# Merged last output parts, a power for the reciprocal root, weight remainders on VectorE, head chains first, buffers moved

## The chip, the cores and the metric

One core of a Trainium2 chip runs the whole program in one launch. The metric is the device time of an execution in microseconds (us). The engines are TensorE (PE, with its weight loads PEld), VectorE (DVE), ScalarE (ACT), GpSimd (POOL) and SyncE (SP, which issues most DMAs). Tiles lie in SBUF; matmuls write PSUM banks of 512 float32 a partition.

## The reference, cut to what matters

Two transformer blocks on one sequence of 512 tokens, width 1024, in float32.

```python
# first block
xn = rmsnorm(h, norm_mix_g)
proj = xn @ w_in                      # q, k, v (512 each), u, gate (512 each), 8 forget logits
log_f = log_sigmoid(proj[..., -8:] + b_forget)
c = cumsum(log_f, axis=1)             # logits = q k / 8 + c_i - c_k, causal; softmax; times v: 8 heads
u, vg = gelu(uv)                      # vg: rmsnorm in groups of 64, mixed in chunks of 128 tokens
h = h + concat(att, u * mixed) @ w_out
h = h + conv_ffn(rmsnorm(h, norm_ffn_g))      # up to 2 x 2816, causal conv of 3, silu(g) * a, down
x = rmsnorm(h, norm_final_g)
# second block
h = modulate(rmsnorm(x), shift, scale)        # shift, scale, gates = silu(c) @ w_ada + b_ada
# latent attention (8 heads of 96) and banded attention with relative bias (8 heads of 64)
x = x + g_a * (concat(o_mla, o_ca) @ w_out)
x = x + g_m * conv_ffn(modulate(rmsnorm(x)))
```

## The kernel before, in words

Activations are kept feature-major as 8 tiles of 128 features x 512 tokens. Every product is computed in three matmuls: each operand is split into a rounded part (`hi`, or `h`) and a remainder (`lo`, or `l`), and hi·hi, hi·lo and lo·hi are added up in PSUM. A triple of matmuls 512 wide stands for one 128 x 128 block of weights.

**Weights.** `make_plan` (L270) lists all pieces of weights in the order in which they are used, each up to 128 x 1024. `load_split` (L327) loads one (SP's queue), casts it to `whi` on ACT (L340) and subtracts to get `wlo` (L341), on POOL where the plan says `pool=True`, else on DVE. There are 3 buffers for the raw pieces, 4 for `whi`, 4 for `wlo`; `prefetch` asks for a piece two pieces ahead of its use. In the first block `w_v` is on DVE; `w_g1` (3 pieces), `w_qk` tiles 0, 4, 1, 5 (one piece each), `w_g0` (2), `w_u` (4) and the other four of `w_qk` are on POOL. `gemm_fm` uses the weights as the stationary operand, `gemm_tm` uses the activations as the stationary one and the weights as the moving one.

**Order.** TensorE's order is written by the program: it runs in the order in which the code emits matmuls. On the other engines a scheduler orders what is ready, by the order of emission unless a priority is given. Work is emitted by generators that yield an estimate of their TensorE time; a `Fill` runs generators until a given estimate is used up. `attention` (L609) emits per step: the scores of one strip of 128 queries, half of the filler, the transposes of the strip before, the other half, the values of the strip before that. Filler is the projections still to do, the spatial gating and the output product; a second `Fill`, `bg`, emits gating work for DVE, POOL and ACT.

**First block, start.** `v`, then `g1` (gate columns and the forget logits), then `qk0`. From the logits ACT and DVE make log f (L1183 to L1194). `cumulate` (L1196) sums it over tokens in 8 matmuls and writes `cum` on ACT and DVE (L1202, L1203). `head(h)` (L1224) splits q and k of one head (`stack`, L650: `qs`, `kh`, `kl`), and picks the head's row out of `cum` with one matmul, whose copy `ch` and masked sum `cm` are the bias of the strips.

**Output product.** `gemm_part` (L393) multiplies two of the eight feature tiles at a time, so x is added to in four parts. `out_tail` (L416) does parts 2 and 3 for the first 256 tokens, then, woven with the norm of those tokens, part 2 and part 3 for the last 256: for each of 8 output tiles 6 matmuls of part 2 and a DVE addition to x (L837, second block L914), later 6 of part 3 and another. Part 3 needs the last pair of heads, which is marked ready in halves as `mix[3, 0]` and `mix[3, 1]`.

**Norms.** `norm_steps` sums squares with 8 small matmuls, calls `rstd` (L501), spreads the result over partitions with `to_rows` (4 matmul records), then `norm_apply` scales. `rstd` is called six times: for each half of the two feed-forward norms and twice in `stats` (L864) between the blocks. It does two DVE operations (L506, L507) and on POOL one (L510) and three Newton rounds of four (L515, L517 twice, L519).

**Memory.** In SBUF, from low to high: descriptor scratch of 16384 bytes a partition, constants, `wraw`, `whi`, `wlo` (4096 bytes a buffer), the activations `act` (8 x 4096), x (8 x 2048), small tiles `sm` (4928 in all, of which 16 of 32 bytes for `rstd`), `acc` (4 x 1024), and above them the pools of a stage: in the feed-forward stages `gh` and `gl`, the 44 operands of the down product, 2048 bytes each.

Of the kernel before, what the change touches and what calls it, by code (L numbers as in the profile page):

```python
# [10 lines left out]
F32 = mybir.dt.float32  # L11
# [8 lines left out]
P = 128  # L20
# [203 lines left out]
LOOK = 2  # L224
HALVES = (slice(0, 256), slice(256, 512))


class Kernel:
# [41 lines left out]
    def make_plan(self):  # L270
        i, plan = self.i, []

        def fm(name, tiles, kt0=0, nk=KT, pool=False, last=None):
            for n in tiles:
                for p in self.fm_pieces(i[name], n, kt0, nk):
                    plan.append((p, pool, None))
            if last:
                plan[-1] = plan[-1][:2] + (last,)

        def tm(name, n, nk=KT, pool=True, last=None, per=None):  # L280
            for p in self.tm_pieces(i[name], n, nk, per):
                plan.append((p, pool, None))
            if last:
                plan[-1] = plan[-1][:2] + (last,)

        def parts(name, dest):
            for p in range(4):
                for g in range(2):
                    plan.append((i[name][p, g], False, dest.get((p, g))))
# [37 lines left out]
    def load_split(self, src, pool, dest):  # L327
# [87 lines left out]

    def out_tail(self, w, mix, evac, evac_last, norm_a):  # L416
# [6 lines left out]
        yield from weave(norm_a, chain(self.gemm_part(w, 2, mix, evac, b, hl2),  # L423
                                       self.gemm_part(w, 3, mix, evac_last, b, hl3, lambda: (3, 1) in mix)))
# [76 lines left out]
    def rstd(self, ms, scale, bias, pool=True):  # L501


        nc = self.nc
        x, y, a, r = (self.sm.tile([P, 2], F32, tag="rstd" + nm, name="rstd", bufs=4) for nm in "xyar")
        nc.vector.tensor_scalar(out=x, in0=ms, scalar1=scale, scalar2=bias, op0=ALU.mult, op1=ALU.add)  # L506
        nc.vector.tensor_scalar(out=y.bitcast(I32), in0=x.bitcast(I32), scalar1=-0.5,  # L507
                                scalar2=float(0x5F3759DF), op0=ALU.mult, op1=ALU.add)
        g = nc.gpsimd if pool else nc.vector
        g.tensor_scalar(out=x, in0=x, scalar1=-0.5, scalar2=None, op0=ALU.mult)  # L510
        cols = (slice(0, 1), slice(1, 2))
        for j in range(3):
            out = r if j == 2 else y
            if pool:
                g.tensor_tensor(out=a, in0=y, in1=y, op=ALU.mult)  # L515
                for c in cols:
                    g.tensor_scalar(out=a[:, c], in0=a[:, c], scalar1=x[:, c], scalar2=1.5, op0=ALU.mult,  # L517
                                    op1=ALU.add)
                g.tensor_tensor(out=out, in0=a, in1=y, op=ALU.mult)  # L519
            else:  # L520
                for c in cols:
                    g.scalar_tensor_tensor(out=a[:, c], in0=y[:, c], scalar=x[:, c], in1=y[:, c],
                                           op0=ALU.mult, op1=ALU.mult)
                g.scalar_tensor_tensor(out=out, in0=a, scalar=1.5, in1=y, op0=ALU.add, op1=ALU.mult)
        return r
# [248 lines left out]
    def run(self):  # L774
# [9 lines left out]
        self.accp = self.pool("acc", 4)  # L784
        self.psn = 0
# [38 lines left out]
        nc.gpsimd.dma_start(out=self.pos, in_=i["pos"])  # L824

# [167 lines left out]
    def block1_mix(self, xn, x, evac, evac_last, norm_a):  # L993
# [143 lines left out]
        def qk(pr):  # L1137
            def ev(n, ps, cs):
                if n < 4:
                    qf[pr] = two.tile([P, 512], F32, tag="qf", name="qf")  # L1140
                    nc.vector.scalar_tensor_tensor(out=qf[pr], in0=ps, scalar=-0.125, in1=rrow,
                                                   op0=ALU.mult, op1=ALU.mult)
                else:
                    kf[pr] = two.tile([P, 512], F32, tag="kf", name="kf")
                    nc.vector.tensor_tensor(out=kf[pr], in0=ps, in1=rrow, op=ALU.mult)
# [37 lines left out]
        nc.scalar.activation(out=la, in_=lf, func=AF.Abs)  # L1183
        nc.scalar.activation(out=la, in_=la, func=AF.Exp, scale=-1.0)
        nc.scalar.activation(out=la, in_=la, func=AF.Ln, bias=1.0)

        lf2 = self.pp.tile([P, 4, 64], F32, tag="p", name="lf2")
        nc.gpsimd.memset(lf2, 0.0)
        lfh, lfl = (stk.tile([P, 4, 64], F32R, tag="st", name="lf" + z) for z in "hl")
        for o in (0, 32):  # L1190
            nc.vector.scalar_tensor_tensor(out=lf2[:, :, o:o + 8], in0=lf, scalar=0.0, in1=la, op0=ALU.min,
                                           op1=ALU.subtract)
        nc.vector.tensor_copy(lfh, lf2)
        nc.vector.tensor_tensor(out=lfl, in0=lf2, in1=lfh.bitcast(F32), op=ALU.subtract)  # L1194
# [488 lines left out]
```

## Time and profile before

| | |
|---|---|
| median of 3 runs | 1263.24 us (1260.85, 1263.3, 1263.24) |
| the profiled execution | 1260.37 us, its span 1258.7 us |
| TensorE busy | 1210.9 us, 96% of the span, 6730 matmul records |
| VectorE, ScalarE, GpSimd busy | 810.2, 537.5, 207.2 us |
| mean granted TensorE clock | 0.986 |
| first block up to its feed-forward stage | about 0 to 243 us |
| feed-forward stage of the first block | about 243 to 613 us |
| second block up to its feed-forward stage | about 613 to 890 us |
| feed-forward stage of the second block | about 890 to 1258 us |

A row of the timeline gives the start, the length, the engine, the line, what is written from what, and in brackets the idle time of the engine before it with what ended it. Lengths of matmuls overlap, as they are pipelined; the distance of their starts is their rate. PEclk is the granted clock: 1.00 is 2.4 GHz, 0.50 is 1.2 GHz.

### The profile page before, as it was taken

The numbers are of one execution on the slowest core, as the hardware profiler recorded it, in microseconds if no ns is written. First come the engines' busy times: TensorE is split into PE (matmuls) and PEld (weight loads), VectorE is DVE, ScalarE is ACT, GpSimd is POOL, SyncE is SP. The second block draws the span as 40 slices with busy tenths as digits, with TensorE's granted clock in tenths as the row PEclk, the third lists the DMA queues.
The fourth block names the chain that finished last, engine by engine and source line by source line (L and its number), as shares of the span: only waits on it lengthen the run. The fifth ranks groups of instructions, "written<-read, shape, count | busy, mean of one in ns | idle before, by whom it ended". The sixth has DMA issues, their size and how long they took to land.

```text
span 1258.7 us, 17548 instructions
## 1 busy us (share of the span) xinstructions
PE 1210.9 (96%) x6730; PEld 1050.3 (83%) x6730; DVE 810.2 (64%) x1550; ACT 537.5 (43%) x964; POOL 207.2 (16%) x281
## 2 busy tenths in 40 slices
PE   9969999999999999999898999899999999999998
PEld 6868878898888888888898987789888888888887
DVE  6456877788778887533566889766676665563321
ACT  5435544454434443223344556664554444442110
POOL 2655700410000000000354342300400000000000
PEclk9979999999999999999999999999999999999999
DMA  7211221236565656533121221100142222233330
GB/s 236 86 65 51 85 84 43 76 118 191 182 196 200 201 196 189 168 104 113 56 68 55 69 96 59 52 23 29 34 134 101 99 87 99 101 92 101 115 111 17
DMA packets 40035, 131.59 MB, mean 105 GB/s; under 512 B 4608, under 2 KB 5504, under 8 KB 39952
## 3 DMA queue, kind: packets, MB, share of 16 engines
q1 hardware_dynamic: 31536, 102.64, 25.0%
q10 hardware_dynamic: 8208, 27.27, 6.7%
q8 instruction: 52, 0.85, 0.3%
q0 software_dynamic: 208, 0.57, 0.2%
q14 instruction: 31, 0.25, 0.1%
HBM read 128.37 MB, written 2.10 MB: 104 GB/s over the span
## 4 chain that ended last, share of the span: by engine, by line
PE 81%; DVE 8%; POOL 6%; ACT 3%; issue 2%; DMA 1%; SPq 0%; POOLq 0%; ACTq 0%; DVEq 0%
PE mm L362 72%; PE s L362 4%; PE o L362 3%; PE s L598 2%; POOL wlo L341 2%; DVE wlo L341 1%; DVE kl L663 1%; POOL gelu L1072 1%; DMA x<-in_xT_dram 1%; ACT p L589 1%; POOL gelu L1073 0%; DVE s L585 0%; DVE uv L1077 0%; PE s L689 0%; POOL sqg L1085 0%
## 5 line engine op out<-in xcount | busy, mean ns | idle before, releaser
L362 PE MATMUL mm<-xnh,whi 128*128 128x512 f32 (+1 forms) x832 | 313.0, 376 | 0.1
L362 PE MATMUL mm<-xnl,whi 128*128 128x512 f32 (+1 forms) x832 | 311.7, 375 | 0.4 <-POOL xnl L554 0.4
L362 PE MATMUL mm<-xnh,wlo 128*128 128x512 f32 (+1 forms) x832 | 311.4, 374 | 0.0
L340 ACT CAST whi<-wraw 128x1024 fp32r<-128x1024 f32 (+4 forms) x194 | 191.9, 991 | 270.3 <-PE mm L362 242.8
L341 DVE TENSOR_TENSOR wlo<-wraw,whi 128x1024 fp32r<-128x1024 f32 (+3 forms) x166 | 190.6, 1157 | 168.9 <-ACT whi L340 168.3
L362 PEld LDWEIGHTS mm<-xnh,wlo 128*128 128x128 f32 x832 | 157.4, 189 | 28.0
L362 PEld LDWEIGHTS mm<-xnh,whi 128*128 128x128 f32 x832 | 157.4, 189 | 27.8 <-issue 0.4
L362 PEld LDWEIGHTS mm<-xnl,whi 128*128 128x128 f32 x832 | 157.5, 189 | 27.6 <-POOL xnl L554 0.6
L362 PE MATMUL mm<-gh,whi 128*128 128x512 f32 (+1 forms) x384 | 143.0, 372 | 1.1 <-DVE x L927 0.6
L362 PE MATMUL mm<-gh,wlo 128*128 128x512 f32 (+1 forms) x384 | 142.0, 370 | 0.0
L362 PE MATMUL mm<-gl,whi 128*128 128x512 f32 (+1 forms) x384 | 140.9, 367 | 0.0
L723 DVE SCALAR_TENSOR_TENSOR cv<-mm,cols,cv 128x510 f32<-128x510 f32 (+1 forms) x176 | 130.4, 745 | 2.6 <-ACT cv L721 1.2
L362 PE MATMUL mm<-whi,xnh 128*128 128x256 f32 (+3 forms) x304 | 96.6, 318 | 2.4 <-ACT vv L1036 1.6
L362 PE MATMUL mm<-whi,xnl 128*128 128x256 f32 (+3 forms) x304 | 94.0, 309 | 0.1
L362 PE MATMUL mm<-wlo,xnh 128*128 128x256 f32 (+3 forms) x304 | 93.8, 309 | 0.2 <-DVE wlo L341 0.2
L988 DVE CUSTOM_DVE_ANT_0 wada<-wada,cs,cols 128x1024 f32<-128x1024 f32 x48 | 61.5, 1280 | 34.9 <-DMA wada<-in_w_ada_dram 34.9
L362 PEld LDWEIGHTS mm<-gh,wlo 128*128 128x128 f32 x384 | 72.1, 188 | 13.5
L362 PEld LDWEIGHTS mm<-gh,whi 128*128 128x128 f32 x384 | 72.3, 188 | 13.1 <-DVE x L927 0.8
L362 PEld LDWEIGHTS mm<-gl,whi 128*128 128x128 f32 x384 | 72.1, 188 | 12.9
L362 PE MATMUL mm<-mix,whi 128*128 128x256 f32 (+1 forms) x288 | 75.9, 352 | 4.3 <-ACT vm L1551 2.6
L589 ACT ACTIVATE p<-s,st 128x128 f32<-128x128 f32 (+1 forms) x96 | 50.7, 528 | 64.6 <-DVE st L585 49.3
L738 ACT ACTIVATE cv<-cv 128x512 f32<-128x512 f32 x44 | 27.8, 632 | 116.4 <-DVE cv L723 116.3
(313 smaller groups left out, 1930.8 us busy)
## 6 DMA issues: line engine op xcount, KB each, us to landing
wraw<-in_w_up_dram SPq DMA_DIRECT2D x88, 512.0 KB, 3.5
wada<-in_w_ada_dram ACTq DMA_DIRECT2D x48, 512.0 KB, 3.7
wraw<-in_w_down_dram SPq DMA_DIRECT2D x32, 512.0 KB, 3.5
wraw<-in_w_out_dram SPq DMA_DIRECT2D x16, 512.0 KB, 3.3
wraw<-in_w_down_dram SPq DMA_DIRECT2D x16, 384.0 KB, 3.2
wraw<-in_w_qk_dram SPq DMA_DIRECT2D x8, 512.0 KB, 3.5
wraw<-in_w_v_dram SPq DMA_DIRECT2D x8, 256.0 KB, 4.9
x<-in_xT_dram SPq DMA_DIRECT2D x8, 256.0 KB, 6.6
```

The source lines that it names most:

```text
L340: nc.scalar.copy(hi[:, :n], raw[:, :n])
L341: (nc.gpsimd if pool else nc.vector).tensor_tensor(out=lo[:, :n], in0=raw[:, :n], in1=hi[:, :n].bitcast(F32), op=ALU.subtract)
L362: self.nc.tensor.matmul(out, lhsT, rhs, start=start, stop=stop, **kw)
L589: nc.scalar.activation(out=p[:, :nk], in_=s[:, :nk], func=AF.Exp, bias=st[:, len(parts) - 1:len(parts)], scale=-1.0, accum_out=hd["sums"](qi))
L598: self.nc.tensor.transpose(s[:, c], p[:, c], self.ident)
L663: nc.vector.tensor_tensor(out=kl[o], in0=k[a], in1=kh[a].bitcast(F32), op=ALU.subtract)
L723: nc.vector.scalar_tensor_tensor(out=t[:, d:], in0=ps[:, :512 - d], scalar=w[2 - d], in1=t[:, d:], op0=ALU.mult, op1=ALU.add)
L738: nc.scalar.activation(out=gate, in_=gate, func=AF.Silu)
L988: nc.vector.tensor_tensor_reduce(out=w, in0=w, in1=self.cs, scale=1.0, scalar=self.col("b_ada_2", n), op0=ALU.mult, op1=ALU.add, accum_out ...
L1072: nc.gpsimd.tensor_tensor(out=t, in0=v, in1=v, op=ALU.mult)
```

## The change

1. **Merged parts.** In `out_tail` parts 2 and 3 of the last 256 tokens become one product: 12 matmuls for each output tile, then one addition to x. It starts when `mix[3, 1]` is marked.
2. **Power for rstd.** `rstd` becomes one DVE operation and one POOL operation, a power with exponent -0.5.
3. **VectorE remainders.** `wlo` of `w_g1`, `w_g0` and `w_qk` tiles 0, 4, 1, 5 is computed on DVE: 9 pieces.
4. **Priority.** The evacuations of q and k, log f (L1183 to L1194), the two writes of `cum` and the preparation of each head of the first block are emitted with a priority 40 places ahead of their own.
5. **Moved buffers.** Each buffer of `whi` and `wlo` is 1088 elements instead of 1024, pieces of token-major weights narrower than 384 columns start 48 elements (192 bytes) into it, a pad of 16 elements lies at the start of `acc`, and the descriptor scratch is 8192 bytes.

```diff
+SKEW, GPAD = 192, 16
+AHEAD = 40
...
         def tm(name, n, nk=KT, pool=True, last=None, per=None):
+            skew = SKEW // 4 if n < 384 else 0
             for p in self.tm_pieces(i[name], n, nk, per):
-                plan.append((p, pool, None))
+                plan.append((p, pool, None, skew))
...
         tm("w_v", 512, pool=False, per=1)
-        tm("w_g1", 264)
-        fm("w_qk", [0, 4], pool=True)
-        fm("w_qk", [1, 5], pool=True)
-        tm("w_g0", 256)
+        tm("w_g1", 264, pool=False)
+        fm("w_qk", [0, 4])
+        fm("w_qk", [1, 5])
+        tm("w_g0", 256, pool=False)
...
-            hi = self.whi.tile([P, 1024], F32R, tag="whi", name="whi")
-            lo = self.wlo.tile([P, 1024], F32R, tag="wlo", name="wlo")
+            hi = self.whi.tile([P, 1088], F32R, tag="whi", name="whi")[:, skew:]
+            lo = self.wlo.tile([P, 1088], F32R, tag="wlo", name="wlo")[:, skew:]
...
+    def gemm_parts(self, parts, x, evac, cs, hls, ready):
+        while not ready():
+            yield 0
+        todo = [(hl, q, k) for p, hl in zip(parts, hls) for q, k in enumerate(PARTS[p])]
+        for n in range(KT):
+            g, j = divmod(n, 4)
+            ps = self.bank()
+            o = ps[:, cs]
+            for m, (hl, q, k) in enumerate(todo):
+                hi, lo = hl[g]
+                ws = slice((2 * j + q) * P, (2 * j + q + 1) * P)
+                xh, xl = (t[:, cs] for t in x[k])
+                self.mm(o, hi[:, ws], xh, m == 0, False)
+                self.mm(o, hi[:, ws], xl, False, False)
+                self.mm(o, lo[:, ws], xh, False, m == len(todo) - 1)
+                yield 650 * (cs.stop - cs.start) // 512
+            evac(n, ps, cs)
...
-        yield from weave(norm_a, chain(self.gemm_part(w, 2, mix, evac, b, hl2),
-                                       self.gemm_part(w, 3, mix, evac_last, b, hl3, lambda: (3, 1) in mix)))
+        yield from weave(norm_a, self.gemm_parts((2, 3), mix, evac_last, b, (hl2, hl3), lambda: (3, 1) in mix))
...
     def rstd(self, ms, scale, bias, pool=True):
-        nc = self.nc
-        x, y, a, r = (self.sm.tile([P, 2], F32, tag="rstd" + nm, name="rstd", bufs=4) for nm in "xyar")
...
+        r = self.sm.tile([P, 2], F32, tag="rstd", name="rstd", bufs=4)
+        self.nc.vector.tensor_scalar(out=r, in0=ms, scalar1=scale, scalar2=bias, op0=ALU.mult, op1=ALU.add)
+        self.nc.gpsimd.tensor_tensor(out=r, in0=r, in1=self.nhalf, op=ALU.pow)
         return r
...
         self.accp = self.pool("acc", 4)
+        nc.gpsimd.memset(self.accp.tile([P, GPAD], F32, tag="pad", name="pad", bufs=1), 0.0)
...
+        self.nhalf = c.tile([P, 2], F32, name="nhalf")
+        nc.gpsimd.memset(self.nhalf, -0.5)
...
             def ev(n, ps, cs):
-                if n < 4:
...
+                with self.tc.high_priority(offset=AHEAD):
+                    if n < 4:
...
-        nc.scalar.activation(out=la, in_=lf, func=AF.Abs)
...
+        with self.tc.high_priority(offset=AHEAD):
+            nc.scalar.activation(out=la, in_=lf, func=AF.Abs)
...
-            nc.scalar.copy(cum, cp)
-            nc.vector.tensor_tensor(out=cum[32:64], in0=cp[32:64], in1=cum[32:64].bitcast(F32),
-                                    op=ALU.subtract)
+            with self.tc.high_priority(offset=AHEAD):
+                nc.scalar.copy(cum, cp)
+                nc.vector.tensor_tensor(out=cum[32:64], in0=cp[32:64], in1=cum[32:64].bitcast(F32),
+                                        op=ALU.subtract)
...
             def f(_):
+                fill.upto(f"qk{h // 2}") if h > 1 else None
+                with self.tc.high_priority(offset=AHEAD):
+                    return prepare(h)
+
+            def prepare(h):
                 pr, odd = divmod(h, 2)
-                fill.upto(f"qk{pr}") if pr else None
...
-    nc = _bacc.Bacc("TRN2", target_bir_lowering=False, num_devices=1)
+    nc = _bacc.Bacc("TRN2", target_bir_lowering=False, num_devices=1, dynamic_dma_scratch_size=8192)
```

## Rows read from the trace of the kernel before

**Rows 1.** The page: engines' busy time, and the granted clock in 40 slices.
```profile
PE 1210.9 (96%) x6730; PEld 1050.3 (83%) x6730; DVE 810.2 (64%) x1550; ACT 537.5 (43%) x964; POOL 207.2 (16%) x281
...
PEclk9979999999999999999999999999999999999999
```

**Rows 2.** Waits of PE, whole span: who waited for whom, us, times, longest.
```profile
PE s L598 <- ACT p L589: 10.1, 9, 2.4
PE mm L362 <- DVE cum L1203: 9.7, 1, 9.7
...
PE r L362 <- POOL rstd L519: 2.5, 1, 2.5
...
PE mm L362 <- POOL rstd L519: 1.3, 1, 1.3
PE mm L362 <- DVE x L914: 1.3, 1, 1.3
```

**Rows 3.** Timeline of PE around the wait for `cum`.
```profile
60.33 0.22 PE L362 MATMUL mm<-tri,lfl 128*64 128x128 f32 x1
...
73.75 0.79 PE L362 MATMUL mm<-cum,pick 64*128 64x512 f32 x1 [9.72 <-DVE cum L1203]
```

**Rows 4.** Stretches: length, busy time of each engine, PEclk, DMA share, GB/s.
```profile
64.00:73.70 9.70, 0.03 (x1) 0.00 (x0) 9.02 (x16) 4.71 (x7) 7.62 (x6) 0.63 0.18 57
73.70:80.20 6.50, 6.45 (x15) 4.76 (x16) 3.66 (x3) 0.59 (x1) 3.15 (x2) 0.50 0.30 102
...
609.30:612.70 3.40, 3.40 (x18) 3.40 (x17) 2.45 (x6) 2.38 (x5) 0.65 (x1) 0.50 0.02 5
```

**Rows 5.** Timeline of DVE from the first gate to `cum`.
```profile
41.85 0.43 DVE L1077 SCALAR_TENSOR_TENSOR uv<-gelu,uv 128x256 f32<-128x256 f32 x1 [0.49 <-ACT gelu L1076]
...
45.05 2.01 DVE L1077 SCALAR_TENSOR_TENSOR uv<-gelu,uv 128x256 f32<-128x256 f32 x1 [0.54 <-ACT gelu L1076]
...
59.66 2.48 DVE L660 TENSOR_TENSOR qs<-qf,qs 64x512 fp32r<-64x512 f32 x1 [1.03 <-ACT qs L659]
...
68.32 3.53 DVE L663 TENSOR_TENSOR kl<-kf,kh 64x512 fp32r<-64x512 f32 x2 [0.35 <-ACT kh L662]
71.87 1.10 DVE L660 TENSOR_TENSOR qs<-qf,qs 64x512 fp32r<-64x512 f32 x1
73.01 0.68 DVE L1203 TENSOR_TENSOR cum<-mm,cum 32x512 fp32r<-32x512 f32 x1
```

**Rows 6.** The same stretch: two remainders on POOL, and all of them.
```profile
44.12 2.65 POOL L341 TENSOR_TENSOR wlo<-wraw,whi 128x1024 fp32r<-128x1024 f32 x1
...
59.20 2.40 POOL L341 TENSOR_TENSOR wlo<-wraw,whi 128x1024 fp32r<-128x1024 f32 x1 [3.27 <-ACT whi L340]
...
L341 POOL TENSOR_TENSOR wlo<-wraw,whi 128x1024 fp32r<-128x1024 f32 (+2 forms) x8 | 18.5, 2308 | 7.6 <-ACT whi L340 7.5
```

**Rows 7.** Lines of DVE, whole span: remainders of 1024 columns.
```profile
L341 DVE TENSOR_TENSOR wlo<-wraw,whi 128x1024 fp32r<-128x1024 f32 x137 | 166.8, 1228 | 118.8 <-ACT whi L340 118.2
```

**Rows 8.** Timelines of PE and DVE at the end of the first output product.
```profile
231.49 1.00 PE L362 MATMUL o<-vv,pt 128*128 128x64 f32 x8
...
232.53 0.42 DVE L681 TENSOR_TENSOR att<-o,sums 128x256 f32<-128x256 f32 x1 [0.69 <-PE o L362]
...
242.06 0.98 PE L362 MATMUL mm<-mix,wsplit 128*128 128x256 f32 x6 [2.09 <-DVE x L837]
```

**Rows 9.** Timelines of DVE and POOL in `rstd` between the blocks.
```profile
604.20 1.23 DVE L341 TENSOR_TENSOR wlo<-wraw,whi 128x1024 fp32r<-128x1024 f32 x1
...
604.38 1.12 POOL L510 TENSOR_SCALAR rstd<-rstd 128x2 f32<-128x2 f32 x1 [343.18 <-DVE rstd L507]
...
608.63 0.19 POOL L519 TENSOR_TENSOR rstd<-rstd 128x2 f32<-128x2 f32 x1
```

**Rows 10.** Stretches of 512-wide matmuls: up product, then down product (columns as Rows 4).
```profile
300.00:400.00 100.00, 100.00 (x443) 82.84 (x442) 80.64 (x112) 41.95 (x56) 0.00 (x0) 1.00 0.59 191
500.00:590.00 90.00, 90.00 (x395) 73.89 (x394) 39.58 (x57) 27.45 (x43) 0.00 (x0) 1.00 0.43 131
```

More of the change, by code (lines that the diff above doesn't have):

```diff
@@ L275, in fm @@
                 for p in self.fm_pieces(i[name], n, kt0, nk):
-                    plan.append((p, pool, None))
+                    plan.append((p, pool, None, 0))
             if last:
-                plan[-1] = plan[-1][:2] + (last,)
+                plan[-1] = plan[-1][:2] + (last, 0)
         def tm(name, n, nk=KT, pool=True, last=None, per=None):
+            skew = SKEW // 4 if n < 384 else 0
             for p in self.tm_pieces(i[name], n, nk, per):
-                plan.append((p, pool, None))
+                plan.append((p, pool, None, skew))
             if last:
-                plan[-1] = plan[-1][:2] + (last,)
+                plan[-1] = plan[-1][:2] + (last, 0)
         def parts(name, dest):
@@ L288, in parts @@
                 for g in range(2):
-                    plan.append((i[name][p, g], False, dest.get((p, g))))
+                    plan.append((i[name][p, g], False, dest.get((p, g)), 0))
         def ffn(up, down, last=None):
@@ L325, in make_plan, with load_split @@
         self.ada_left, self.pools, self.before = [], {}, []
-    def load_split(self, src, pool, dest):
+    def load_split(self, src, pool, dest, skew):
         nc, n = self.nc, src.shape[-1]
@@ L1138, in ev @@
             def ev(n, ps, cs):
-                if n < 4:
[L1140 to L1145, printed above, removed]
+                with self.tc.high_priority(offset=AHEAD):
+                    if n < 4:
+                        qf[pr] = two.tile([P, 512], F32, tag="qf", name="qf")
+                        nc.vector.scalar_tensor_tensor(out=qf[pr], in0=ps, scalar=-0.125, in1=rrow,
+                                                       op0=ALU.mult, op1=ALU.mult)
+                    else:
+                        kf[pr] = two.tile([P, 512], F32, tag="kf", name="kf")
+                        nc.vector.tensor_tensor(out=kf[pr], in0=ps, in1=rrow, op=ALU.mult)
             return self.gemm_fm(i["w_qk"], [pr, 4 + pr], xn, ev)
@@ L1181, in block1_mix @@
         both(pre)
-        nc.scalar.activation(out=la, in_=lf, func=AF.Abs)
[L1184 to L1194, printed above, removed]
+        with self.tc.high_priority(offset=AHEAD):
+            nc.scalar.activation(out=la, in_=lf, func=AF.Abs)
+            nc.scalar.activation(out=la, in_=la, func=AF.Exp, scale=-1.0)
+            nc.scalar.activation(out=la, in_=la, func=AF.Ln, bias=1.0)
+            lf2 = self.pp.tile([P, 4, 64], F32, tag="p", name="lf2")
+            nc.gpsimd.memset(lf2, 0.0)
+            lfh, lfl = (stk.tile([P, 4, 64], F32R, tag="st", name="lf" + z) for z in "hl")
+            for o in (0, 32):
+                nc.vector.scalar_tensor_tensor(out=lf2[:, :, o:o + 8], in0=lf, scalar=0.0, in1=la,
+                                               op0=ALU.min, op1=ALU.subtract)
+            nc.vector.tensor_copy(lfh, lf2)
+            nc.vector.tensor_tensor(out=lfl, in0=lf2, in1=lfh.bitcast(F32), op=ALU.subtract)
         def cumulate():
```

19 lines of the change are left out of this document (removed).

## The prediction

> **What bounds the kernel now.** I read the page first: PE is busy 96% of the span at full clock but for one slice [rows 1], so only three things can save time: PE's idle time (some 48 of 1258.7 us), half-clock stretches, and the rate of the matmuls themselves. Then the waits of PE, whose longest entries say where to look [rows 2]: one wait of 9.7 us for `cum`, 10.1 us in nine pieces for the exponentials of the strips, and short waits for x (L914; L837 in [rows 8]) and `rstd` (L519) at the joints between stages. Then the timelines around these. The windows show what idle time costs beyond itself: after the wait for `cum` PE works 6.5 us at half clock, and 0.4 us after the wait for `rstd` between the blocks it works 3.4 us at half clock [rows 4]. Last, the windows of both feed-forward products, which have no idle time, for the rate of matmuls [rows 10].
>
> **The wait for `cum`: remainders on VectorE and priority.** The reader is to see that the wait has nothing to do with TensorE's work. The 8 matmuls of `cumulate` start their last one at 60.33; the matmul that picks a row waits from 64.03 to 73.75 [rows 3], and ends when DVE has done L1203, at 73.01 to 73.69. That is one instruction of 0.68 us, which stood behind qs, two kl and qs in DVE's order, and they stood behind late work [rows 5]. What made DVE late is in the same rows: the gate's L1077 takes 0.43 us alone, but 2.01 us while POOL subtracts a remainder (44.12 to 46.77); qs takes 2.48 us beside the remainder of 59.20 to 61.60, and 1.10 us later [rows 5, 6]. The gate chain alternates DVE and POOL, and POOL does eight remainders there, 18.5 us [rows 6]. The change takes nine remainders from POOL (most of these eight) and gives DVE nine: six of 1024 columns at 1.23 us [rows 7] and three of 792, 792 and 528, by width 0.95, 0.95 and 0.63, together 9.9 us. DVE gets back the stretched parts: 1.58 us at 45.05, 1.38 us at 59.66, and about two thirds of the 3.53 us of the two kl, so some 5 us in the rows I quote. `cum` also passes ahead of the gate's Newton steps and scalings.
>
> So `cum` can be there by about 63: 60.4, 0.6 us on ACT, 0.7 us on DVE, and one instruction in front. That is before PE wants it at 64.03, and 9.72 us go, with the loss at half clock: 6.45 us of busy time would have taken half, 3.2 us [rows 4]. Together 12.9. Late next is the first head's split (kf, then qs and two kl, about 4 us of DVE without POOL beside it), which PE wants some seven triples (4.8 us) after the pick; with up to four remainders in the same stretch of DVE I leave 2 us for it: **-10.9**. Bounds: -12.9, and 0 if the wait merely moves to the scores.
>
> Against the change speaks one more row: POOL's L510 took 1.12 us beside a remainder on DVE, where its neighbour takes 0.19 [rows 9]. Nine remainders on DVE can so hold POOL up by some 0.9 us each, 8 us; POOL is given back nine of 2.3 us, 21 us, so this changes who is late by little, and is in the 2 us.
>
> The evacuations and the other heads' preparation have the priority too. The strips' waits for exponentials [rows 2] could shrink or grow by it: I take 0, with 3 us to either side.
>
> **Merged parts.** At the end of the first product PE waits 2.09 us for a bank that L837 has yet to empty [rows 8], in the second 1.3 us for L914 [rows 2]. In the half concerned DVE makes 16 additions, one for 6 matmuls (0.72 us); merged, 8, one for 12 matmuls (1.44 us): these waits go. TensorE's matmuls stay the same in number. The price is in the first block: part 2 now also waits for the last half pair, so it no longer fills TensorE while the last values are finished. From the values' end (231.49 and eight records, about 232.3) to the end of att at 232.95 [rows 8] is 0.65 us, then two transposes; their split on ACT and DVE (some 1.1 us) is covered by the nine matmuls of the three feature tiles that are ready. I take 0.8 us lost. In the second block the last pair is long there. So **-1.3** in the first, **-1.3** in the second; bounds -2.1 and +1 for the first.
>
> **Power for rstd.** POOL's chain runs from 604.38 to 608.82, 4.4 us in ten operations, and PE waits 2.5 us for its last [rows 2, 9]; in the second block 1.3 us. In the other four calls the matmuls that the code places between (4000 units, 13 steps of three 256-wide matmuls, about 4.7 us) hide it: nothing there. The trace has no power. Bounds: 0.19 us, as another operation on 2 columns [rows 9], and 4.4 us, as the whole chain. It is one operation on the same tile, so I take the value near the first, under 1 us; the remainder on DVE at 604.20 holds it till 605.43 in any case, and PE wants the result at 606.43. Both waits go: -2.5 and -1.3. The half clock at 609.30 [rows 4], 3.4 us of work, would give back 1.7 if it follows from that gap; behind it the norm's own steps are late already, so I count half: **-4.7** in all, bounds 0 and -5.5.
>
> **Moved buffers.** The up product issues 441 matmuls in 100 us, 226.8 ns each; the down product, of the same width, 393 in 90 us, 229.0 ns (the counts less two under way at the edges) [rows 10]. By the sizes in the code, `act` lies a multiple of 256 bytes above the weights, the down product's operands 64 bytes off that (`sm` is 4928 bytes). After the change `sm` is 4544, the pad adds 64, the buffers are 17 x 256: every operand is then at a multiple of 256 from the weights, as the up product's is. If that offset is the cause, 924 down matmuls of full width gain 2.2 ns: **-2.0**. The cause isn't in the rows, so the other end is the up product's 1920 losing as much, +4.2. The 192 bytes under narrow pieces I take at 0, with 1.5 to either side.
>
> By the Trainium skill (TensorE: Matmul & The Clock Gate, Step-by-step: what each phase is for), TensorE has two independent read ports, so that loading weights doesn't disturb the streaming operand; placement then changes nothing. The two rates of rows 10 don't decide it, as the products also differ in their tiles.
>
> **Sum.** 10.9 + 2.6 + 4.7 + 2.0 = 20.2. The profiled execution took 1260.4 (span 1258.7 and 1.7 around it), so 1240.2; the median of the runs is 2.9 above it: **1243**.
>
> **Rivals.**
> - *The early wait changes its place.* DVE gets 9.9 us in a stretch where it is the late engine, and head 0's scores or the first gates' weights become what PE waits for. For it: DVE was busy 9.0 of the 9.7 us of that wait [rows 4], and the order of an engine is fixed before the run. Against it: half of that busy time is stretch. If 3 us of the 12.9 are gained, 1243 + 8 = 1251.
> - *Placement changes nothing*, all else as forecast: 1245. The rule of the Trainium skill named above would have it so.
> - *The power is slow, and the kernel slower.* Six calls, covers of about 4.7 us in four, some 2.5 at `stats`' first and 6 at its second: 27 us. With X us a power, the loss is 6X - 27, and it must eat 20 us: from X = 7.8 on the kernel is slower than before, at 10 us 1243 + 33 + the 3.8 of removed waits, about 1280. For it: a function that no row shows. Against it: all POOL operations on 2 columns take about 0.2 us.
>
> **How the numbers follow.** Forecast 0.58 (its own range 1236 to 1248), placement without effect 0.17, the early wait moved 0.17, slow power 0.04; 0.04 for a placement that costs more than all else gains. The low end: 12.9 + 3.4 + 5.5 + 2.0 + 3 is 26.8, so 1236; a little more if narrow pieces gain. The high end is the moved wait with the up product slowed: 1255. Range 1235 to 1255. A measurement here tells 0.2%, 2.5 us, from no change; within that lies a moved wait with several other terms failing: 0.05. Slower: 0.08. Faster: 0.87.
>
> **What would show it.** In the profile of the changed kernel: no wait of PE for L1203 above 1 us and full clock from 60 to 100 us; POOL's L341 fewer by nine; no PE wait for `rstd`, POOL's power below 1 us; no wait for L837 at the end of the first product, and a gap below 1 us before the transposes of the last att; the down product at 227 ns. Wrong would be: a wait of over 5 us for scores, kl or `wlo` between 60 and 110 us; a power over 3 us; the up product above 228 ns; more waits for exponentials than 13 us.

## The result, and the profile after

The changed kernel takes **1247.56 us** (median of 4 runs, 1246.03 to 1248.05) where the kernel before takes 1263.27 beside it: ratio 0.9878, 95% interval 0.9861 to 0.9895. Run once more among the experiments (`after2`, below) it gave 0.9907 (0.9886 to 0.9929), so a kernel of the study has to differ from it by some 3 us before medians alone tell them apart. For smaller effects I use the traces. The profiled execution of one kernel, `x_nomerge`, took 1697 us at a mean granted clock of 0.654, where the others have about 0.99, and is left out of all that follows.

The page of the profiled execution (1248.05 us, span 1245.1), against [rows 1]: PE's busy time fell by 4.3 us and the span by 13.6, so 9.3 us are idle time gone. In the clock row the third slice, at 7 tenths before, is at 8, and one later slice fell to 8. POOL lost 34 us.

```profile
PE 1206.6 (97%) x6730; PEld 1048.7 (84%) x6730; DVE 803.4 (65%) x1538; ACT 536.7 (43%) x963; POOL 173.0 (14%) x202
...
PEclk9989999999999999999998999999999999999999
```

PE's waits in it, against [rows 2]. To be seen: `cum` is still there with 3.8 of 9.7 us, `rstd` is gone, and two entries are new, `nt` with 3.2 us and `xnl` with 1.3.

```profile
PE s L603 <- ACT p L594: 10.4, 9, 2.4
PE mm L1600 <- DVE ca L1427: 4.8, 1, 4.8
PE mm L367 <- DVE cum L1215: 3.8, 1, 3.8
PE mm L367 <- DVE nt L550: 3.2, 1, 3.2
...
PE mm L367 <- DVE xnl L562: 1.3, 1, 1.3
```

PE has 6730 records in both traces, so its n-th record can be set against the n-th: the difference of their starts is the changed kernel's lead there. What a stage gains is the lead at its end less that at its beginning. Beside it stands what the prediction gave to that stage:

| records of PE | stage | lead at its end, us | gained | forecast |
|---|---|---|---|---|
| 0 to 600 | start, `cum`, first head | 8.10 | 8.1 | 10.9 |
| 600 to 1050 | strips of the first block | 9.36 | 1.3 | 0 |
| 1050 to 1200 | the last att transposes | 8.53 | -0.8 | -0.8 |
| 1200 to 1500 | end of the output product, start of the feed-forward network | 7.02 | -1.5 | 2.1 |
| 1500 to 3000 | up and down product | 7.91 | 0.9 | 1.0 |
| 3000 to 3450 | `rstd` between the blocks | 11.31 | 3.4 | 3.4 |
| 3450 to 3600 | latents, the wait for `ca` | 9.83 | -1.5 | 0 |
| 3600 to 4800 | strips of the second block | 11.51 | 1.7 | 0 |
| 4800 to 5250 | end of the second output product, second norm | 12.76 | 1.3 | 2.6 |
| 5250 to 6729 | up and down product | 13.55 | 0.8 | 1.0 |

The -1.5 at `ca` and the 1.7 behind it are no effects of the change: in `after2`, the same program, the wait was 4.2 us in place of 4.8 and the half clock after it lasted 3.4 us in place of 6.8, and its lead differs from the first execution's by 1.8 us there and by 0.4 us at the end. At the table's marks up to record 3450 the two executions agree within 0.11 us. The 1.3 us at the strips of the first block are of the same kind: the kernel before works 3.4 us at half clock at 186, the changed one at none there.

**What is left of the wait for `cum`.** The timelines of DVE, POOL and PE around it, against [rows 3, 5]:

```profile
61.86 0.17 DVE L520 SCALAR_TENSOR_TENSOR sst<-sst 128x16 f32<-128x16 f32 x1
...
62.49 2.49 DVE L1105 TENSOR_TENSOR uv<-uv,ss 128x256 f32<-128x256 f32 x4
65.01 1.10 DVE L665 TENSOR_TENSOR qs<-qf,qs 64x512 fp32r<-64x512 f32 x1
66.14 0.68 DVE L1215 TENSOR_TENSOR cum<-mm,cum 32x512 fp32r<-32x512 f32 x1
...
62.99 3.70 POOL L1107 TENSOR_TENSOR uv<-uv,gg_row 128x256 f32<-128x256 f32 x4 [6.19 <-DVE uv L1105]
...
66.88 0.79 PE L367 MATMUL mm<-cum,pick 64*128 64x512 f32 x1 [3.76 <-DVE cum L1215]
```

ACT is done with its part at 61.87, so L1215 could have run then. In front of it stand three Newton steps of the gate, the gate's four scalings L1105 (2.49 us beside the gate's own multiplications L1107 on POOL: the two that lie wholly beside L1107 take 0.95 and 0.94 us, the first, ahead of it, 0.43; the like L1427 takes 1.43 for four without them) and qs: the priority did not put `cum` ahead of any of them. The remainders still on POOL don't explain what is left: in `y_dve` below, which has none there, the wait is 3.8 us as well.

**What is new at the feed-forward network.** PE's first matmuls there, and two of the eight multiplications by the spread-out `rstd`:

```profile
231.57 0.28 PE L367 MATMUL mm<-xnh,wlo 128*128 128x256 f32 x1
235.03 0.35 PE L367 MATMUL mm<-xnh,whi 128*128 128x256 f32 x1 [3.18 <-DVE nt L550]
...
228.75 0.87 DVE L550 SCALAR_TENSOR_TENSOR nt<-x,cols,mm 128x256 f32<-128x256 f32 x2
...
234.02 0.86 DVE L550 SCALAR_TENSOR_TENSOR nt<-x,cols,mm 128x256 f32<-128x256 f32 x2
```

Three matmuls run, the fourth waits 3.18 us. It reads the same activations as the first, so it does not seem to wait for these (experiment 6 puts it to the test). In the compiled program it writes the second feature tile of the up product, in PSUM bank 5, and bank 5 still holds the row of `rstd`, which L550 reads until 234.88. In the kernel before the row lay in bank 6. Behind that wait the clock falls. The stretches at half clock, against [rows 4] (13.7 us behind `cum` and 3.4 behind `rstd` there), and the matmul rates against [rows 10]:

```profile
65.10:71.90 6.80, 5.02 (x11) 3.71 (x12) 6.04 (x5) 0.58 (x1) 5.62 (x4) 0.50 0.25 73
...
235.80:239.20 3.40, 3.40 (x18) 3.40 (x17) 1.59 (x1) 0.00 (x0) 0.51 (x1) 0.50 0.21 61
607.90:611.30 3.40, 3.38 (x16) 3.09 (x16) 1.60 (x7) 0.90 (x3) 2.96 (x5) 0.51 0.15 54
...
300.00:400.00 100.00, 100.00 (x443) 82.86 (x442) 79.71 (x110) 41.47 (x56) 0.00 (x0) 1.00 0.58 191
495.00:575.00 80.00, 80.00 (x355) 66.28 (x354) 36.69 (x56) 25.29 (x41) 0.00 (x0) 1.00 0.45 135
```

Over the span, but for its last 3 us, half clock (granted 0.50, 1.2 GHz) fell from 34.1 to 27.3 us. The down product now issues 353 matmuls in 80 us, 226.6 ns each, as the up product does; it was 229.0.

The remainders left on POOL, against the eight of [rows 6] and 28 in all before, and the power, against the chain of [rows 9]:

```profile
L346 POOL TENSOR_TENSOR wlo<-wraw,whi 128x1024 fp32r<-128x1024 f32 (+2 forms) x19 | 44.6, 2354 | 23.6 <-ACT whi L345 23.6
...
L529 POOL TENSOR_TENSOR rstd<-rstd,nhalf 128x2 f32<-128x2 f32 x6 | 5.1, 853 | 360.4 <-DVE rstd L528 360.4
...
596.25 1.60 POOL L529 TENSOR_TENSOR rstd<-rstd,nhalf 128x2 f32<-128x2 f32 x1 [342.06 <-DVE rstd L528]
...
596.08 1.23 DVE L346 TENSOR_TENSOR wlo<-wraw,whi 128x1024 fp32r<-128x1024 f32 x1
```

The mean of 0.85 us hides two cases: five powers take 0.68 to 0.73 us, and the one between the blocks, for which PE had waited before, takes 1.60 us beside a remainder on DVE.

### The profile page after: what moved, and what is told of

It is laid out like the page before. It is cut to its first block, busy times and chain, and to the rows that moved or that the text cites. A ratio compares the mean times of both kernels' runs of the same rounds, so it can differ in the third digit from the quotient of the medians.

```text
span 1245.1 us, 17452 instructions
## 1 busy us (share of the span) xinstructions
PE 1206.6 (97%) x6730; PEld 1048.7 (84%) x6730; DVE 803.4 (65%) x1538; ACT 536.7 (43%) x963; POOL 173.0 (14%) x202
## 4 chain that ended last, share of the span: by engine, by line
PE 83%; DVE 8%; POOL 4%; ACT 3%; issue 2%; DMA 1%; SPq 0%; POOLq 0%; ACTq 0%; DVEq 0%
PE mm L367 73%; PE s L367 4%; PE o L367 3%; PE s L603 2%; POOL wlo L346 1%; DVE wlo L346 1%; DMA x<-in_xT_dram 1%; ACT p L594 1%; ACT whi L345 0%; PE s L694 0%; DVE s L590 0%; DVE kl L668 0%; DVE nw L522 0%; PE mm L1639 0%; POOL gelu L1081 0%
## 5 line engine op out<-in xcount | busy, mean ns | idle before, releaser
L346 DVE TENSOR_TENSOR wlo<-wraw,whi 128x1024 fp32r<-128x1024 f32 (+4 forms) x175 | 200.6, 1155 | 167.1 <-ACT whi L345 166.2
L367 PEld LDWEIGHTS mm<-gh,whi 128*128 128x128 f32 x384 | 72.4, 189 | 13.6 <-DVE x L936 0.8
L367 PEld LDWEIGHTS mm<-gh,wlo 128*128 128x128 f32 x384 | 72.4, 189 | 11.9
```

Of the source, the lines that this page charges most:

```text
L346: (nc.gpsimd if pool else nc.vector).tensor_tensor(out=lo[:, :n], in0=raw[:, :n], in1=hi[:, :n].bitcast(F32), op=ALU.subtract)
L367: self.nc.tensor.matmul(out, lhsT, rhs, start=start, stop=stop, **kw)
```

## The experiments

Ratios are to the kernel before, run beside each. "Lead" is again that of PE's records, against the changed kernel. A trace is that of one execution, not always of the median one: the profiled one of `x_pow2` took 1250.24 us (median 1253.42), that of `y_dve` 1236.95 (median 1240.43).

**1. The remainders back on POOL (`x_pool9`).**

```
-        tm("w_g1", 264, pool=False)
-        fm("w_qk", [0, 4])
-        fm("w_qk", [1, 5])
-        tm("w_g0", 256, pool=False)
+        tm("w_g1", 264)
+        fm("w_qk", [0, 4], pool=True)
+        fm("w_qk", [1, 5], pool=True)
+        tm("w_g0", 256)
```

> The changed kernel with the nine remainders of the first gates and of qk0 and qk1 given back to POOL; the priority, merged parts, power and moved buffers stay. Theory (the remainders on POOL stretched DVE's work in front of cum): the wait of PE for cum grows from 3.8 us to 7 to 9 us, with 3 us more at half clock, and the kernel takes 5 to 8 us more than the changed one, 1253 to 1256. Rival (the priority alone brought cum forward, the remainders only change engines): the wait stays between 3 and 5 us and the time within 2 us of 1247.6.

Measured: 1251.02 us, ratio 0.9934 (0.9909 to 0.9959). The wait is back in full:

```profile
PE mm L367 <- DVE cum L1215: 9.8, 1, 9.8
```

At the pick it is 6.9 us behind the changed kernel; the kernel before is 6.87 behind. So the nine remainders are the whole gain at that place, 0.9 us of it earlier, by record 150, which the forecast had not counted. The theory on the wait holds and the rival falls, though the time grew by some 3 us and not by 5 to 8. DVE's busy time is 801.9 us here and 803.4 with the nine, 9.9 us of work, on DVE: on POOL they had cost DVE nearly as much. In the end it lies only 3.2 us behind, because by chance its row of `rstd` falls into bank 6: it has no wait for `nt`, and makes good 4.7 us there; that is why its time stayed below the expectation.

**2. No priority (`x_ahead0`).**

```
-AHEAD = 40
+AHEAD = 0
```

> The changed kernel with the priority's offset 0 in place of 40, so that the gate's, the evacuations' and the heads' chains have no priority. Theory (the remainders did most of it): the wait for cum is 4 to 6 us and the kernel takes 0 to 3 us more than 1247.6. Rival (the priority did it): the wait for cum is 8 to 10 us, and the time 1253 to 1257. A third case: the priority costs more at the strips than it gives at cum, then the waits for exponentials (10.4 us in nine now) fall below 9 us and the time is below 1247.

Measured: 1247.05 us, ratio 0.9893 (0.9872 to 0.9914), no difference from the changed kernel.

```profile
PE mm L367 <- DVE cum L1215: 3.6, 1, 3.6
```

The wait for `cum` is the same, and DVE's order in front of L1215 still ends with the Newton steps, L1105 and qs. The waits for exponentials are 9.5 us, 0.9 less, but the lead at the end is 1.4 us less: at the strips of the first block this execution loses 2.4 us, with 6.8 us of half clock at 176 that the changed kernel's has not. The priority does nothing that these runs can tell from such differences.

**3. Newton in place of the power (`x_newton`).**

```
-        self.nc.vector.tensor_scalar(out=r, in0=ms, scalar1=scale, scalar2=bias, op0=ALU.mult, op1=ALU.add)
-        self.nc.gpsimd.tensor_tensor(out=r, in0=r, in1=self.nhalf, op=ALU.pow)
+        ...
-SKEW, GPAD = 192, 16
+SKEW, GPAD = 192, 48
```

> The changed kernel with the Newton iteration for rstd in place of the power (the pad is 192 bytes in place of 64, so that all matmul operands keep their offsets modulo 256 bytes). Theory (the forecast's steps): PE waits again about 2.5 us for rstd between the blocks and 1.3 us in the second block, and the kernel takes 3 to 5 us more, 1250.5 to 1252.5. Rival (the gain between the blocks is given back at the wait for ca at 661.5, which grew from 4.0 to 4.8 us with 3.4 us more at half clock behind it): the wait for ca is 4.0 us again with 3.4 us at half clock, and the kernel takes 0 to 2 us more.

Measured: 1254.16 us, ratio 0.9946 (0.9925 to 0.9968): 5 to 9 us more than the changed kernel, above the upper end of either expectation.

```profile
PE r L367 <- POOL rstd L543: 2.4, 1, 2.4
PE mm L367 <- POOL rstd L543: 1.9, 2, 1.4
```

By the lead: 1.6 us at the end of the first output product, 3.0 between the blocks, 3.9 at the second norm, where 6.8 us of half clock follow at 887; at `ca` 1.5 us come back by the clock. The 1.6 us are a wait that the kernel before did not have: with the parts merged, the chain of ten operations no longer fits between its matmuls. So the power is worth more in the changed kernel than in the one before, though how much of it is the clock's these runs don't separate.

**4. No merged parts (`x_nomerge`).**

```
-        yield from weave(norm_a, self.gemm_parts((2, 3), mix, evac_last, b, (hl2, hl3), lambda: (3, 1) in mix))
+        yield from weave(norm_a, chain(self.gemm_part(w, 2, mix, evac, b, hl2),
+                                       self.gemm_part(w, 3, mix, evac_last, b, hl3, lambda: (3, 1) in mix)))
```

> The changed kernel with the output parts of the second half one after the other as before. Theory (the forecast): the wait for the bank that L846 empties comes back with about 2 us at the end of the first product, and 1.3 us for x in the second; 2 to 3 us more than 1247.6. Rival (merging only moved the wait to the start of the feed-forward network, where PE waits 3.2 us for norm_apply and works 3.4 us at half clock): the start of the feed-forward network has no wait above 1 us and no half clock, and the kernel takes 1247 or less.

Measured: 1247.75 us, ratio 0.9903 (0.9881 to 0.9924), as the changed kernel. No trace of it is compared, so nothing follows from it on where the waits went. Its row of `rstd` too lies in bank 5. Experiment 11 repeats the question where the bank does not blur it.

**5. The changed kernel again (`after2`).** No edit.

> The changed kernel itself, to stand beside the other kernels of this study on the same chip. From its ratio of 0.9878: 1243 to 1249.

Measured: 1248.66 us, ratio 0.9907 (0.9886 to 0.9929).

**6. The row of rstd in another bank (`x_bank`).**

```
-            rows = self.to_rows(r, self.bank(self.side))
+            rows = self.to_rows(r, self.bank("s" if self.side == "mm" else self.side))
```

> The changed kernel, but the row of rstd that norm_apply reads is put in a PSUM bank of the pool s and not of the pool mm. Theory (the wait of 3.2 us at the start of the feed-forward network is for a bank: the row of the first half lay in bank 5, which the second feature tile of the up product takes, and the eight multiplications L550 hold it to their end): no wait above 1 us there, no half clock behind it, 4 to 5 us less than the changed kernel, beginning at that place of the trace. Rival (PE waits there for the values xn themselves, which the merged parts make late): the wait stays at 2 to 3 us, and the time within 1 us of the changed kernel's.

Measured: 1247.70 us, ratio 0.9901 (0.9878 to 0.9923).

```profile
235.81 0.39 PE L367 MATMUL mm<-xnh,whi 128*128 128x256 f32 x1 [1.98 <-DVE x L846]
...
234.80 0.62 DVE L554 TENSOR_TENSOR xnl<-nt,xnh 128x256 fp32r<-128x256 f32 x1
235.34 0.74 DVE L846 TENSOR_TENSOR x<-mm,x 128x256 f32<-128x256 f32 x2
```

The wait for `nt` is gone, so it was for the bank and not for xn. But the tiles behind the row moved up by one bank, bank 5 now holds the last tile but one of the output product, and PE waits 1.98 us until DVE adds it to x behind the norm's multiplications; the 3.4 us of half clock stay. 1.2 us of the 4 to 5 are gained in that stage, and 1.6 us lost at the strips, with 3.4 us of half clock at 179, eat them. The mechanism was right, the cure was not.

**7. More matmuls in front of the first head (`x_cumfill`).**

```
         cumulate()
-        for _ in range(2):
+        for _ in range(5):
```

> The changed kernel with five in place of two helpings of other matmuls between cumulate and the first head (range(2) to range(5): 4.5 us more of TensorE work before the first pick). Its row of rstd falls into bank 7, so by the theory on the bank the 3.2 us at the feed-forward network go as well. Theory (the 3.8 us left of the wait for cum are DVE's lateness alone and other matmuls cover it): no wait for cum above 1 us, full clock from 60 to 100 us, 5 to 7 us less at that place, and with the bank 9 to 12 us less in all. Rival (the wait moves on to the first scores, or the strips get later and their waits longer, since the qk1 filler is used up earlier): less than 3 us gained by 130 us of the trace.

Measured: 1245.57 us, ratio 0.9883 (0.9857 to 0.9909). No wait for `cum` and no half clock before 117 us; the lead is 5.3 us at record 450. By record 600 it is -1.2: the theory is right on `cum` and the rival on what follows. DVE and POOL at that place, and PE's wait:

```profile
110.71 5.56 DVE L668 TENSOR_TENSOR kl<-kf,kh 64x512 fp32r<-64x512 f32 x2
...
110.10 5.62 POOL L346 TENSOR_TENSOR wlo<-wraw,whi 128x1024 fp32r<-128x1024 f32 x2
...
116.98 1.04 PE L367 MATMUL o<-vv,pt 128*128 128x64 f32 x6 [2.89 <-DVE pt L605]
```

Two kl that take 1.38 us elsewhere (at 60.45 in the changed kernel) take 5.56 us beside two remainders of `w_u` on POOL, and `pt` stands behind them. Its row of `rstd` is in bank 7, and as in `x_bank` a wait for L846 (2.3 us) took the place of that for `nt`.

**8. The power everywhere (`x_pow2`).**

```
     def newton(self, out, x, y, a):
-        ...
+        nc = self.nc
+        nh = self.nhalf[:, 0:1]
+        nc.gpsimd.tensor_tensor(out=out, in0=x, in1=nh.to_broadcast(list(x.shape)), op=ALU.pow)
```

> The changed kernel with every Newton iteration (gates, q and k heads, latents) replaced by the one power on POOL. Its row of rstd falls into bank 6, so by the theory on the bank the 3.2 us at the feed-forward network go. Theory (DVE's ten steps of Newton in front of ca stretch to 2.3 us each time while POOL subtracts a remainder): the wait for ca falls from 4.8 us to below 2 us and the half clock behind it to 3.4 us or less, 3 to 6 us less there; with the bank 7 to 11 us less in all. Rival (the power stands behind a remainder of 2.4 us on POOL, and the wait stays): 4 us or more for ca, and only the bank's 5 us are gained.

Measured: 1253.42 us, ratio 0.9948 (0.9931 to 0.9965), slower than the changed kernel though its bank is right (4.8 us gained there).

```profile
PE s L598 <- ACT p L589: 14.2, 10, 3.3
PE mm L1595 <- DVE ca L1422: 6.7, 2, 4.7
```

The rival holds for `ca`: its wait stays. The time is lost at the strips: 4.3 us between records 450 and 600, and 3.7 at those of the second block. That the power is late there, behind other work of POOL, is likely but was not taken apart further.

**9. The kernel before with moved buffers alone (`b_pad`).**

```
+        nc.gpsimd.memset(self.accp.tile([P, 48], F32, tag="pad", name="pad", bufs=1), 0.0)
...
-    nc = _bacc.Bacc("TRN2", target_bir_lowering=False, num_devices=1)
+    nc = _bacc.Bacc("TRN2", target_bir_lowering=False, num_devices=1, dynamic_dma_scratch_size=8192)
```

> The kernel before, with 192 bytes of pad (and the smaller scratch memory that makes room for it) as its only edit: the operands of the down products and of the output products then stand at a multiple of 256 bytes from the weights, where they stood 64 bytes off. Theory (the place sets the rate): the down product takes 226 to 227 ns per matmul of 512 columns in place of 229, 1 us less in each block, and 2 us less in all (1258.5 where the kernel before takes 1260.5). Rival (the rule of the Trainium skill, TensorE: Matmul & The Clock Gate, Step-by-step: what each phase is for, by which the weights and the streaming operand have ports of their own; the other edits changed the rate): 229 ns as before and the same time.

Measured: 1258.60 us, ratio 0.9983 (0.9974 to 0.9992), 2.1 us less. The window of [rows 10] in it:

```profile
500.00:590.00 90.00, 90.00 (x399) 74.51 (x397) 39.83 (x58) 27.50 (x43) 0.00 (x0) 1.00 0.45 137
```

397 in place of 393 matmuls in 90 us: 226.7 in place of 229.0 ns. Against the kernel before the lead grows by 0.9 us in the first down product and by 0.8 in the second. Only places were changed, so place alone moved this rate, by 2.3 ns a matmul; the pad moved the operands by 192 bytes both in themselves and against the weights, and which of the two counts is not shown. By the Trainium skill (TensorE: Matmul & The Clock Gate, Step-by-step: what each phase is for) weight loads and the streaming operand use read ports that don't disturb each other. That section says nothing of where operands lie; the rival's reading of it, that place changes nothing, does not hold here.

**10. All remainders on VectorE (`y_dve`), and with it more matmuls before the first head (`y_dve_f4`).**

```
-        def tm(name, n, nk=KT, pool=True, last=None, per=None):
+        def tm(name, n, nk=KT, pool=False, last=None, per=None):
...
-        fm("w_qk", [2, 6], pool=True)
-        fm("w_qk", [3, 7], pool=True)
+        fm("w_qk", [2, 6])
+        fm("w_qk", [3, 7])
```

and in `y_dve_f4` also

```
         cumulate()
-        for _ in range(2):
+        for _ in range(4):
```

> The changed kernel with all weight remainders that are still POOL's (w_u, qk2, qk3, and the latent stage's w_cq, w_cv, w_ck) on VectorE. Theory (a remainder on POOL costs VectorE as much as doing it: DVE's busy time fell by 6.8 us when nine went over): DVE's busy time stays within 10 us of 803 though it does some 19 remainders more, the Newton steps in front of ca take 0.2 us each, PE's wait for ca falls from 4.8 us to 1 to 3 us, and the kernel takes 2 to 6 us less than the changed one. Rival (DVE is the late engine of the strips, and 19 remainders of 1.23 us, 23 us, make its work later): the waits for exponentials grow from 10.4 us to 14 or more and the kernel takes 2 to 6 us more.

> As y_dve, with four in place of two helpings of matmuls between cumulate and the first head; the row of rstd falls into bank 7, which the up product's first tiles don't take. Theory: no wait for cum above 1 us; without POOL's remainders of w_u beside the first strips the 3.7 us that five helpings lost there (PE for pt, 98 to 117 us) are below 1 us; no bank wait at the feed-forward network; with y_dve's gain at ca 8 to 14 us less than the changed kernel, 1233 to 1240. Rival (the strips are bound by their own chain, whatever POOL does): the lead of 4 to 5 us at the first head is lost again by 125 us of the trace, and the time is 1241 or more.

Measured: `y_dve` 1240.43 us, ratio 0.9843 (0.9827 to 0.9859); `y_dve_f4` **1230.45 us, ratio 0.9761 (0.9748 to 0.9775)**, faster than both kernels by far more than the spread. Both gain more than expected. The rival of `y_dve` falls: waits for exponentials are 9.6 us. So does that of `y_dve_f4`: its lead at the first head is kept. Its wait for `cum` is 1.1 us, just above the mark. Its page has DVE at

```profile
PE 1202.8 (97%) x6730; PEld 1045.6 (85%) x6730; DVE 810.8 (66%) x1551; ACT 538.8 (44%) x969; POOL 134.2 (11%) x183
```

803.4 us with 19 remainders on POOL, 810.8 with none: some 25 us of work went over, and DVE is 7.4 us busier. Why is seen at `ca`. First DVE and POOL in the changed kernel, then DVE in `y_dve`:

```profile
659.85 0.17 DVE L521 TENSOR_TENSOR nw<-nw,ssc 128x16 f32<-128x16 f32 x1
660.06 2.28 DVE L522 SCALAR_TENSOR_TENSOR nw<-nw 128x16 f32<-128x16 f32 x1
...
662.58 0.17 DVE L521 TENSOR_TENSOR nw<-nw,ssc 128x16 f32<-128x16 f32 x1
662.79 2.29 DVE L522 SCALAR_TENSOR_TENSOR nw<-nw 128x16 f32<-128x16 f32 x1
...
659.89 2.42 POOL L346 TENSOR_TENSOR wlo<-wraw,whi 128x1024 fp32r<-128x1024 f32 x1 [0.52 <-ACT whi L345]
662.71 2.34 POOL L346 TENSOR_TENSOR wlo<-wraw,whi 128x1024 fp32r<-128x1024 f32 x1 [0.40 <-ACT whi L345]
```

```profile
655.29 0.17 DVE L522 SCALAR_TENSOR_TENSOR nw<-nw 128x16 f32<-128x16 f32 x1
...
655.92 0.18 DVE L522 SCALAR_TENSOR_TENSOR ssc<-nw 128x16 f32<-128x16 f32 x1
656.13 1.43 DVE L1427 TENSOR_TENSOR ca<-ca,ssc 128x256 f32<-128x256 f32 x4
```

A step of 0.17 us that starts inside a remainder of POOL ends 0.03 us after that remainder does (662.31 and 662.34, 665.05 and 665.08): it is not slowed in proportion, it stands until POOL is done. By the Trainium skill (SBUF — State Buffer, Who interferes with whom) the two engines share one pair of ports as an exclusive lock; these rows agree. PE's wait for `ca`, 4.8 us, is gone from `y_dve`, with the half clock behind it: 7.6 us in that stage, 5.8 against `after2`. In `y_dve_f4` some 4 us at `cum` come on top, are still there at record 600 (5.0 us), and its row of `rstd` lies in bank 7 with bank 5 free early, which gives 4.8 us at the feed-forward network. `x_cumfill` had one helping more and POOL's remainders, and lost its lead at the strips; that the remainders made the difference fits the rows there, but one edit between the two was not run. The waits left in `y_dve_f4`:

```profile
PE s L603 <- ACT p L594: 9.2, 8, 2.4
PE mm L367 <- ACT vm L1567: 2.6, 1, 2.6
PE s L694 <- DVE att L686: 1.5, 4, 0.5
PE mm L367 <- DVE xnl L562: 1.3, 1, 1.3
PE mm L367 <- DVE cum L1215: 1.1, 1, 1.1
```

**11. The same without merged parts (`y_f4_nomerge`).** The edit of experiment 4 on `y_dve_f4`.

> As y_dve_f4, but with the output parts of the second half one after the other, as before the change; the row of rstd lies in bank 7, which the up product's first tiles don't take, so that this time no wait for a bank at the feed-forward network hides what merging is worth. Theory (the forecast): the wait of about 2 us for the bank that L846 empties comes back at the end of the first product, less 0.5 us for the transposes of the last att, and 1.3 us for x in the second block; 2 to 4 us more than y_dve_f4, 1232.5 to 1234.5. Rival (merging only exchanges waits): within 1 us of y_dve_f4's 1230.5 in the medians and in the trace behind the start of each feed-forward network.

Measured: 1230.92 us, ratio 0.9767 (0.9742 to 0.9791): the rival's result in the medians, though not in the trace, where `y_dve_f4` is 2.1 us ahead behind the start of the first feed-forward network. The trace tells why:

```profile
PE mm L367 <- DVE x L847: 2.6, 2, 2.0
PE mm L367 <- DVE x L924: 1.4, 1, 1.4
```

Both old waits are back. Merging gains 4.3 us at the start of the first feed-forward network (the 2.0 us of the wait, and 3.4 us of half clock at 227 that it brings), and loses 0.7 at the last att transposes, as forecast. In the second block it only exchanges waits, L924's 1.4 us for the 1.3 us at `xnl`, and there `y_dve_f4` has 3.4 us of half clock at 866 that this kernel has not: 1.9 us back. What the clock does behind a wait of 1.3 or 1.4 us decides the balance there, and it did not do the same behind both. The rest of the balance has nothing to do with the edit: where both kernels issue the same matmuls in the same order, `y_dve_f4` loses 1.8 us at the strips of the first block (3.4 us of half clock at 169) and 1.3 between the blocks (at 600), and gains 1.5 at the strips of the second. So equal medians don't show that merging is worth nothing, and the trace of one pair of executions doesn't show its worth to better than 2 us.

## Why the prediction was right, and where it was not

The sign, the size and the range held (1243 forecast, 1235 to 1255, measured 1247.6). The forecast for the profiled execution was 1240.2 and it took 1248.05: 6.6 us too little gained within the span, 1.3 in what lies around it. The median came out 0.5 us below the profiled execution, not 2.9 above. Part of the agreement is luck: without those 2.9 us the forecast would have been 1240, and against the kernel before, run beside it, the gain is 15.7 us (11.9 in `after2`) where 20.2 were forecast.

- **Wait for `cum`: 8.1 for 10.9.** Right that it has nothing to do with TensorE's work and that POOL's remainders made DVE late; `x_pool9` shows the nine remainders alone bring 6.9 us at the pick. Failed: the step "`cum` also passes ahead of the gate's Newton steps and scalings". It stood behind all of them, with the priority or without (`x_ahead0`). What the forecast took for stretch by remainders alone comes from other work of POOL too: L1105 stretches beside L1107, 0.95 us for 0.43. The first mark of the forecast, no wait above 1 us and full clock, came out wrong; `y_dve_f4` comes to 1.1 us and has no half clock there.
- **The rival of the early wait** did not decide: 3.8 us stayed in place, none moved to scores or weights.
- **Attention priority: 0**, and in the medians of `x_ahead0` no difference was measured.
- **Merged parts, first block: forecast -1.3; measured 2.3 us worse.** The wait for L837 went and the gap at the last transposes cost 0.8, both as forecast (PE waits 0.52 us for att at 218.23). Failed: the question what is late next was put to the transposes alone, not to the first matmuls behind the product. There the row of `rstd` sits in the bank that the second feature tile takes. That the row lands there is not the merging's doing: the assignment differs between kernels that share it (bank 5 in the changed kernel, 6 in `x_pool9`, 7 in `y_dve_f4`). With the bank out of the way (experiment 11) merging gained 3.6 us in that block in one pair of traces, more than forecast, because of the clock.
- **Merged parts and power, second block: 1.3 for 2.6.** `rstd` and L914 no longer hold PE, but L562 does, for 1.3 us: one of the two was exchanged, not removed.
- **Power: 3.4 for 3.4 between the blocks**, 0.68 to 0.73 us in five calls, nearer the lower bound, as chosen. The sixth, the one between the blocks, takes 1.60 us, above the mark of 1 us, and PE does not wait for it all the same. "Nothing there" for the four covered calls is right for the kernel before and not for the changed one: `x_newton` waits up to 1.4 us in one of them. The equal numbers are in part luck. The lead rises by 2.6 us at the wait and by 1.6 where the half clock behind it is gone, of which the forecast counted half; it falls by 1.1 us some 65 matmuls later, at 607.9, where other 3.4 us of half clock stand that the kernel before has not.
- **Moved buffers: 1.7 for 2.0**, and 2.1 by themselves in the kernel before. The 256-wide matmuls at the end of the down product take 120 ns in place of 118, which takes 0.3 us back in the second. The rival that placement changes nothing falls.
- **Slow power** falls: 1.60 us at most where 7.8 were needed.

## What to carry to other kernels

A subtraction of two SBUF tiles that was moved to GpSimd was here hardly taken off VectorE: 28 of them moved back, 35 us of work, made VectorE 9 us busier (1.5 and 7.4) and took 6 us of the wait for `cum` and all of that for `ca` with them, so look for small VectorE operations whose length equals what GpSimd still has to do. Put other matmuls in front of a late result before giving it a priority: two helpings more, with POOL's remainders gone, took the wait from 3.8 to 1.1 us, and a priority of 40 places did nothing; with the remainders on POOL the lead was lost again at the strips (`x_cumfill`). And when a wait goes, read the next matmuls' PSUM banks as well as their operands: which small tile shares a bank with the next stage's first tiles was worth close to 5 us here, and no edit was meant to set it.

## What the runs showed that I had not expected

- One and the same wait has different prices. Behind the 3.8 us for `cum` PE had 6.8 us of half clock in the changed kernel and 3.4 in `x_newton`; behind the 4.8 us for `ca` 6.8 us in the changed kernel and 3.4 in `x_bank`. A difference below 2 us between two traces can be this alone.
- The rate of a matmul of 512 columns depends on where its operands lie: 229.0 ns in the down product with the streaming operand 64 bytes off a multiple of 256 bytes from the weights, 226.7 on it; at 256 columns the sign is the other (118 and 120 ns). Other offsets were not measured.
- Two operations of 0.69 us each on VectorE took 5.56 us beside two GpSimd subtractions of 128 x 1024 (110.10 to 115.72).
